# A max-pool-and-subtract stream with eight-row tiles in three slots instead of six-row tiles in four

## The chip, the cores and the metric

The kernel runs on one core of a Trainium2 chip. The metric is the device time of that core in microseconds; the profile's span, from the first to the last recorded instruction, is some 2 us shorter than the run it was taken in (624.8 us against 626.6 us). Lower is better.

The parts of the core that matter here: VectorE (DVE) does all arithmetic; SyncE (SP) issues the loads and ScalarE (ACT) the stores, each on a queue of its own; sixteen DMA engines, shared by both queues, move the data; TensorE (PE) only passes on a semaphore.

## What is computed

An array of 8 x 64 images of 256 x 256 float32 numbers. Each image is cut into windows of 8 x 8, the maximum of each window is taken, and every element has the maximum of its window subtracted:

```python
def reference(x):
    B, C, H, W = x.shape          # 8, 64, 256, 256
    pH, pW = 8, 8
    oH, oW = H // pH, W // pW
    x_r = x.reshape(B, C, oH, pH, oW, pW)
    pooled = x_r.max(axis=(3, 5))
    upsampled = np.repeat(np.repeat(pooled, pH, axis=2), pW, axis=3)
    return (x - upsampled).astype(np.float32)
```

134.22 MB come in and as much goes out.

## The kernel before

A "row" in this kernel is a strip of eight image lines, 2048 numbers or 8 KB, which holds 32 whole windows and is contiguous in memory. There are 16,384 of them, 128 for each of the 128 partitions. They are worked in tiles: a first tile of four rows per partition, 20 tiles of six, and a last tile of four. A tile of six rows takes for each partition one contiguous run of 48 KB, so one descriptor of the transfer moves 48 KB. The first tile comes in two loads and leaves in two stores, the last one leaves in three.

```python
ROW = 2048
HEAD, HEAD_OUT = [3, 1], [2, 2]
SIZE, TILES = 6, 20
TAIL = [2, 1, 1]
SLOTS = 4
...
    sizes = [sum(HEAD)] + [SIZE] * TILES + [sum(TAIL)]
    last = len(sizes) - 1
    ring = data.tile([P, SLOTS * SIZE * ROW], F32, name="ring")
    tops = data.tile([P, SLOTS * SIZE * oW], F32, name="tops")
```

`ring` is a ring of slots in SBUF, 24 rows or 192 KB per partition. Tile i lies in slot (i - 1) % SLOTS. The subtraction is done in place: a tile is loaded into its slot, changed there, and stored from there, so a slot is taken from the start of a load to the end of the store.

The load queue. A load into a slot that was used before waits until the stores of the tile that lay there have landed (L113 of the profile is the issue of a load):

```python
        for i in range(len(sizes)):
            slot = slot_of(i)
            if landed[slot]:
                nc.sync.wait_ge(stored[slot], 16 * landed[slot])
            for k, (lo, R) in enumerate(cuts(HEAD if i == 0 else [sizes[i]])):
                part = slice(lo * ROW, (lo + R) * ROW)
                nc.sync.dma_start(out=sbuf(i, lo, R), in_=dram(x_rows, i)[:, part]).then_inc(
                    first[k] if i == 0 else loaded[slot], 16
                )
            landed[slot] += len(HEAD_OUT) if i == 0 else 1
```

TensorE turns "this tile has landed" into one step of a single semaphore, `filled`, which the loop on VectorE can wait for with a constant:

```python
        for i in range(1, last):
            turn = (i - 1) // SLOTS + 1
            nc.tensor.wait_ge(loaded[slot_of(i)], 16 * turn).then_inc(filled, 1)
```

The store queue waits for VectorE's `ready` and issues the store (L130):

```python
        for i in range(len(sizes)):
            for lo, R in cuts(HEAD_OUT if i == 0 else TAIL if i == last else [SIZE]):
                part = slice(lo * ROW, (lo + R) * ROW)
                done += 1
                nc.scalar.wait_ge(ready, done)
                nc.scalar.dma_start(out=dram(out_rows, i)[:, part], in_=sbuf(i, lo, R)).then_inc(
                    stored[slot_of(i)] if i + SLOTS <= last else final, 16
                )
```

VectorE: for each tile one reduction over all its windows (L81) and one subtraction per row (L96); the tile counts as ready after the last subtraction. `take` (L75) waits for a semaphore and counts it down.

```python
        nc.vector.tensor_reduce(out=..., in_=..., axis=mybir.AxisListType.XY, op=mybir.AluOpType.max,
        ).then_inc(reduced if nth is None else pooled, 1)
        ...
        for r in range(R):
            sub = nc.vector.tensor_tensor(
                out=wins[:, r],
                in0=wins[:, r],
                in1=maxs[:, r].unsqueeze(1).unsqueeze(3).to_broadcast([P, pH, oW, pW]),
                op=mybir.AluOpType.subtract,
            )
        sub.then_inc(ready, 1)
...
        with nc.vector.Fori(0, TILES) as i:
            slot = i % SLOTS
            take(filled, 1)
            pool_and_subtract(
                ring[:, bass.ds(slot * (SIZE * ROW), SIZE * ROW)],
                tops[:, bass.ds(slot * (SIZE * oW), SIZE * oW)],
                SIZE,
            )
```

Of the kernel before, what the change touches and what calls it, by code (L numbers as in the profile page):

```python
# [1 line left out]

# [4 lines left out]

F32 = mybir.dt.float32
ROW = 2048


HEAD, HEAD_OUT = [3, 1], [2, 2]
SIZE, TILES = 6, 20
TAIL = [2, 1, 1]
SLOTS = 4


@with_exitstack
def kernel(
    ctx: ExitStack,  # L20
    tc: tile.TileContext,
    x: bass.AP,
    out: bass.AP,
):
    nc = tc.nc
    P = nc.NUM_PARTITIONS
    B, C, H, W = x.shape
    pH = pW = 8
    oW = W // pW

    x_rows = x.rearrange("b c (oh ph) w -> (b c oh) (ph w)", ph=pH)
    out_rows = out.rearrange("b c (oh ph) w -> (b c oh) (ph w)", ph=pH)
    sizes = [sum(HEAD)] + [SIZE] * TILES + [sum(TAIL)]
    assert sum(sizes) * P == x_rows.shape[0] and max(sizes) == SIZE
    starts = [P * sum(sizes[:i]) for i in range(len(sizes))]
    last = len(sizes) - 1

    data = ctx.enter_context(tc.tile_pool(name="data", bufs=1))
    ring = data.tile([P, SLOTS * SIZE * ROW], F32, name="ring")
    tops = data.tile([P, SLOTS * SIZE * oW], F32, name="tops")  # L40
    first = [tc.alloc_semaphore(f"first{i}") for i in range(len(HEAD))]
    loaded = [tc.alloc_semaphore(f"loaded{i}") for i in range(SLOTS)]
    stored = [tc.alloc_semaphore(f"stored{i}") for i in range(SLOTS)]
    final = tc.alloc_semaphore("final")
    filled = tc.alloc_semaphore("filled")
    reduced = tc.alloc_semaphore("reduced")
    pooled = tc.alloc_semaphore("pooled")
    ready = tc.alloc_semaphore("ready")

    def slot_of(i):  # L50

        return (i - 1) % SLOTS

    def dram(rows, i):

        n = sizes[i]
        return rows[starts[i] : starts[i] + P * n].rearrange("(p r) d -> p (r d)", r=n)

    def sbuf(i, lo, R):
        at = (slot_of(i) * SIZE + lo) * ROW  # L60
        return ring[:, at : at + R * ROW]

    def top(i, lo, R):
        at = (slot_of(i) * SIZE + lo) * oW
        return tops[:, at : at + R * oW]

    def cuts(parts):
        lo = 0
        for R in parts:
            yield lo, R  # L70
            lo += R

    def take(sem, n):

        nc.vector.wait_ge(sem, n).then_inc(sem, -n)  # L75

    def pool_and_subtract(part, top, R, nth=None):

        wins = part.rearrange("p (r ph ow pw) -> p r ph ow pw", r=R, ph=pH, ow=oW)
        maxs = top.rearrange("p (r ow) -> p r ow", r=R)  # L80
        nc.vector.tensor_reduce(  # L81
            out=maxs if R > 1 else maxs[:, 0],
            in_=(
                wins.rearrange("p r ph ow pw -> p r ow ph pw")
                if R > 1
                else wins[:, 0].rearrange("p ph ow pw -> p ow ph pw")
            ),
            axis=mybir.AxisListType.XY,
            op=mybir.AluOpType.max,
        ).then_inc(reduced if nth is None else pooled, 1)  # L90
        if nth is None:
            take(reduced, 1)
        else:
            nc.vector.wait_ge(pooled, nth)
# [9 lines that stand above are left out]
    with tc.tile_critical(sync_engine=nc.gpsimd.engine, no_gpsimd_drain=True):  # L104

        landed = [0] * SLOTS
# [17 lines that stand above are left out]
        done = n_final = 0  # L124
# [8 lines that stand above are left out]
                n_final += i + SLOTS > last  # L133
        nc.scalar.wait_ge(final, 16 * n_final)


        for k, (lo, R) in enumerate(cuts(HEAD_OUT)):
            nc.vector.wait_ge(first[[a + n >= lo + R for a, n in cuts(HEAD)].index(True)], 16)
            pool_and_subtract(sbuf(0, lo, R), top(0, lo, R), R, k + 1)
# [8 lines that stand above are left out]
        nc.vector.wait_ge(loaded[slot_of(last)], 16 * ((last - 1) // SLOTS + 1))  # L148
        for k, (lo, R) in enumerate(cuts(TAIL)):
            pool_and_subtract(sbuf(last, lo, R), top(last, lo, R), R, len(HEAD_OUT) + k + 1)  # L150


# [1 line left out]
_INS = ['x']  # L154
_OUTS = [((8, 64, 256, 256), 'float32')]


# [23 lines left out]
```

## Time and profile before

| | |
|---|---|
| time, median of 3 runs | 627.52 us (627.07 to 628.71) |
| span of the profiled run | 624.8 us |
| moved, in and out | 268.44 MB, mean 430 GB/s |
| VectorE busy | 560.2 us, of which reductions 276.8 and subtractions 284.1 |
| one reduction of six rows | 12.95 us |
| one subtraction of a row | 2.287 us |
| a load of six rows per partition, issue to landing (median) | 37.9 us |
| a store of six rows per partition, issue to landing (median) | 51.0 us |

The page gives busy time by engine, then forty equal slices of the span: a digit is the busy share of a slice in tenths, and for DMA it is the mean share of the core's sixteen engines; GB/s is what they moved. Lists of waits name the waiting engine and line, what ended the wait, and then the total in us, how often, and the longest. In a table by stretches each row has the stretch, its length, busy time of VectorE and of GpSimd with instruction counts, the granted clock, the DMA share and GB/s. The timeline has start, length, engine, line and operation, and in brackets the idle time before.

### The profile page before, as it was taken

How to read it: one execution, taken by the hardware profiler on the slowest of the kernel's cores; microseconds unless marked ns; L12 is line 12 of the kernel's file. 1: busy time of each engine (PE TensorE's matmuls, PEld its weight loads, DVE VectorE, ACT ScalarE, POOL GpSimd, SP SyncE). 2: the span in 40 equal slices, each digit the busy share in tenths (PEclk: the TensorE clock that was granted, in tenths of full speed). 3: DMA queues.
4: the chain of work that ended last, by engine and by line, in shares of the span. 5: the costliest groups of instructions: out<-in, count | busy, mean ns of one | idle time of the engine just before them, and what ended most of it. 6: DMA issues, size and time to landing. Idle time of an engine off the chain costs nothing. (4 is left out here: it accounts for less than half of the span.)

```text
span 624.8 us, 519 instructions
## 1 busy us (share of the span) xinstructions
DVE 560.2 (90%) x153; POOL 0.2 (0%) x4
## 2 busy tenths in 40 slices
DVE  3899999999999898989898989889898989898991
POOL 0000000000000000000000000000000000000000
DMA  9999999999999999999999999999999999999998
GB/s 369 415 447 413 453 403 453 450 406 453 428 428 450 406 453 441 415 453 419 437 450 406 453 431 425 453 403 453 444 412 453 425 431 447 409 453 432 441 422 350
DMA packets 6913, 268.44 MB, mean 430 GB/s; under 512 B 769, under 2 KB 769, under 8 KB 769
## 3 DMA queue, kind: packets, MB, share of 16 engines
q1 hardware_dynamic: 3312, 134.22, 49.9%
q10 hardware_dynamic: 3600, 134.22, 49.7%
q14 instruction: 1, 0.00, 0.0%
HBM read 134.22 MB, written 134.22 MB: 430 GB/s over the span
## 5 line engine op out<-in xcount | busy, mean ns | idle before, releaser
L81 DVE TENSOR_REDUCE tops<-ring (+2 forms) x25 | 276.8, 11074 | 47.4 <-DVEq L75 36.7
L96 DVE TENSOR_TENSOR ring<-ring,tops (+1 forms) x128 | 284.1, 2287 | 3.3 <-DVEq L75 3.1
L165 POOL MEMSET const-bfloat16-1.0<- 128x1 bf16 x1 | 0.1, 102 | 0.0
L165 POOL MEMSET const-uint8-127<- 128x1 uint8 x1 | 0.1, 102 | 0.0
L165 POOL MEMSET const-float32-0.0<- 128x1 f32 x1 | 0.1, 99 | 0.2 <-issue 0.2
L165 POOL MEMSET const-float32-1.0<- 128x1 f32 x1 | 0.1, 99 | 0.0
## 6 DMA issues: line engine op xcount, KB each, us to landing
ring<-in_x_dram SPq DMA_DIRECT2D x20, 6144.0 KB, 37.9
out_dram<-ring ACTq DMA_DIRECT2D x20, 6144.0 KB, 51.0
out_dram<-ring ACTq DMA_DIRECT2D x3, 2048.0 KB, 24.8
ring<-in_x_dram SPq DMA_DIRECT2D x1, 4096.0 KB, 33.4
ring<-in_x_dram SPq DMA_DIRECT2D x1, 3072.0 KB, 9.8
out_dram<-ring ACTq DMA_DIRECT2D x2, 1024.0 KB, 13.8
ring<-in_x_dram SPq DMA_DIRECT2D x1, 1024.0 KB, 11.9
```

Source lines behind the costliest of these rows:

```text
L81: nc.vector.tensor_reduce(out=maxs if R > 1 else maxs[:, 0], in_=(wins.rearrange("p r ph ow pw -> p r ow ph pw") if R > 1 else wins[:, 0]. ...
L96: sub = nc.vector.tensor_tensor(out=wins[:, r], in0=wins[:, r], in1=maxs[:, r].unsqueeze(1).unsqueeze(3).to_broadcast([P, pH, oW, pW]), op ...
L165: nc = _bacc.Bacc("TRN2", target_bir_lowering=False, num_devices=1)
```

## The change

The tiles between the first and the last have eight rows in place of six, so that each partition's part of one is 64 KB, and there are 15 of them in place of 20. To fit the same 24 rows of SBUF, there are three slots in place of four. The first tile's four rows come in two loads of two rows, in place of three and one. The purpose is to have fewer transfers and larger descriptors, 64 KB in place of 48. Nothing else in the text of the kernel changes; the waits follow from the constants: a load of tile i now waits for the store of tile i - 3.

```diff
-HEAD, HEAD_OUT = [3, 1], [2, 2]
-SIZE, TILES = 6, 20
+HEAD, HEAD_OUT = [2, 2], [2, 2]
+SIZE, TILES = 8, 15
 TAIL = [2, 1, 1]
-SLOTS = 4
+SLOTS = 3
```

## The prediction

> **What bounds the kernel now.** I read the page first (busy shares, slices, queues), then the time by stretches, then the wait lists of VectorE and of the load queue, and last the timeline of both ends. The page alone names two candidates:
>
> ```profile
> span 624.8 us, 519 instructions
> DVE 560.2 (90%) x153; POOL 0.2 (0%) x4
> ...
> DMA  9999999999999999999999999999999999999998
> GB/s 369 415 447 413 453 403 453 450 406 453 428 428 450 406 453 441 415 453 419 437 450 406 453 431 425 453 403 453 444 412 453 425 431 447 409 453 432 441 422 350
> ...
> q1 hardware_dynamic: 3312, 134.22, 49.9%
> q10 hardware_dynamic: 3600, 134.22, 49.7%
> ```
>
> VectorE is busy for 90% of the span, but the sixteen DMA engines are busy for all of it: loads (q1) and stores (q10) share them half and half, 99.6% together. The stretches say the same without the two ends:
>
> ```profile
> 0.00:30.00 30.00, 17.74 (x6) 0.20 (x4) 1.00 0.95 387
> 30.00:600.00 570.00, 531.62 (x143) 0.00 (x0) 1.00 1.00 434
> 600.00:624.80 24.80, 10.83 (x5) 0.00 (x0) 1.00 0.91 391
> ```
>
> The last two columns are the DMA share and GB/s. For 570 us the share is 1.00 at 434 GB/s. All 268.44 MB at that rate take 618.5 us, so of the 624.8 only about 6 us are not transfer at the full rate. The packet records of the trace begin at 1.9 and end at 623.2 with no hole. Who waits for whom:
>
> ```profile
> DVE tops L81 <- DVEq L75: 36.7, 15, 2.7
> DVE tops L81 <- DMA ring<-in_x_dram: 10.7, 1, 10.7
> ...
> SPq L113 <- DMA out_dram<-ring: 547.7, 18, 60.6
> ```
>
> VectorE's wait at L75 is its wait for a load, up to 2.7 us on 15 tiles: it keeps up and waits for data. The load queue waits for stores (L113, `stored`). And yet DMA never idles, since issued stores stand in line: from issue to landing a 6 MB store takes 51.0 us and a load 37.9, where one alone would take 14.5 (6.29 MB at 434). That line is the reserve of four slots. The chain of waits shows 5% only, all VectorE at the end; it does not see transfers, so it is no help here.
>
> **What the Trainium skill says.** "DMA: Bandwidth & Descriptors", section "Where 436 GB/s comes from", gives a ceiling of 435.2 GB/s for the sixteen engines; the 434 above agrees, so there is nothing left in the middle for larger descriptors to win. The same page, "Queues, rings and completion order", says each engine takes turns between the queues that have work; the trace agrees: with both queues full, a 48 KB load descriptor (1.815 us) and a store descriptor alternate, and each transfer takes about twice its time alone. Its section "Anatomy of one DMA" says that a wait for a semaphore is made by the issuing sequencer, not by the DMA engine; so a load whose slot is not free is not in any queue, and an engine can go dry. No wait of that kind ends in an idle DMA in the trace before.
>
> **The change part by part.** *Descriptors.* The packet records have 8 KB in 0.309 us and 48 KB in 1.815 us: 36.8 ps a byte and 8 ns fixed. 2,560 descriptors of 48 KB in each direction become 1,920 of 64 KB, on each engine 320 become 240; 80 x 8 ns = 0.6 us gained.
>
> *VectorE's work* is the same: 128 subtractions at 2.287 us and the same rows reduced. From one reduce to the next of a six-row tile it is 26.32 us (30.75 to 57.07 in the timeline), so eight rows take 35.0. A tile's two transfers take 8 x 2 x 2.416 = 38.7 us (a row of all partitions is 1.0486 MB, 2.416 us at 434 GB/s), so VectorE at 35.0 stays below the DMA. The order of instructions shows no other change than shapes, counts and two more subtractions in the loop's body.
>
> *Slots.* SBUF holds the same 24 rows. In the loop of one slot stand load, VectorE, store and three latencies. I take from the trace: last load packet to reduce 2 us (0.85 from the last engine, plus that the engines end up to 2.2 us apart), last subtraction to first store packet 2 us (1.0 idle, 3.6 under load), last store packet to first packet of the load that waits for it 2.5 us (0.36 to the semaphore, 1.0 to the first packet, and half of the 2.4 us between engines). With full queues the round is 37 + 2 + 35 + 2 + 37 + 2.5 = 115.5 us against 3 x 38.7 = 116. Four slots of six: 27 + 2 + 26.3 + 2 + 27 + 2.5 = 87 against 4 x 29.0 = 116. A reserve of 29 us becomes one of nothing. Holes appear where neither a load nor a store is ready, so I schedule by hand, both queues sharing evenly when both have work:
>
> Start: two rows land at 6.7, VectorE works 7.6 to 25.4 on tile 0. The first eight-row tile lands at 40.6 (sixteen row transfers, 38.7, after 1.9), and VectorE starts on it at 42.6 (before: 30.75). From there VectorE runs tiles 1 to 5 back to back, ending at 77.6, 112.6, 147.6, 182.6, 217.6. Loads 2 and 3 end at 79.3; store 1 runs alone from 79.6 to 98.9, then load 4 may start, at 101.4: hole of 2.5. Load 4 is alone until store 2 at 114.6; store 2 ends 140.0, load 5 at 142.5: hole 2.5. Store 3 ends 181.2, load 6 at 183.7: hole 2.5. Store 4 ends 222.4 with store 5 in line: no hole. Start together, with 0.3 before store 1: 7.8.
>
> Middle: from here stores and loads end within 2 us of each other, and one of them nearly always bridges the other's gap; going on in the same way to tile 14, I find holes of 1.0, 0.9, 0.3 and 0.8: 3.0.
>
> End: load 15 lands at 572.7, VectorE works on it until 609.7. All that DMA has meanwhile is store 14 (19.3) and the four-row load 16 (9.7), done by 602.5. Store 15 begins at 610.7: hole of 8.2. Before, loads end near 588 and two full stores stand in line behind, so no hole.
>
> Sum: 7.8 + 3.0 + 8.2 = 19.0, less 0.6 for descriptors, 18.4 on the span. The time before, 627.5, becomes 645.9, slower by 2.9%.
>
> **The rivals.** *The transfers hide it all:* VectorE still has 3.7 us a tile to spare and some transfer is nearly always open; then only the descriptors count: 627. For it speaks the 99.6%, against it the reserve worked out above and the end, where one tile of VectorE's work is longer than what is left to move. *Every tile has a hole:* loads and stores fall into step, both end together, and each of twelve steady tiles idles for the 2.5 us from store to load: 30 us in place of 3, about 672. For it: both rounds, 115.5 and 116, are equal within my error. Against it: VectorE's spare time lets the next store be in line already. *Large descriptors run faster:* the 36.8 ps a byte at 8 KB and at 48 KB alike speak against more than 1 us, 626.
>
> **Range and chances.** The end's hole is the surest part (it rests on 35.0 us of VectorE against 29.0 of transfers plus latencies), say 5 to 11 us; the start's 4 to 10; the middle 0 to 15. Holes can also be partly bridged where the sixteen engines end at different times, so there is more room below. Low: 636; high: 654. The 2% line is at 640.1, 5.8 below my number, so slower by over 2% gets 0.76, within 2% 0.23, faster 0.01.
>
> **What would show it.** Right: VectorE's first eight-row reduce near 42 us; slices with a DMA digit of 8 or less or GB/s near 380 in the first third and one clear dip near 605 us; DMA share of the two queues together about 97%; VectorE busy again 560 us; shorter times from issue to landing, stores most. Steady stretches at 430 GB/s or more say that the middle costs nothing. Wrong: a span near 625 with all nines (the reserve was not needed), GB/s below 420 in every slice of the middle (holes at each tile), or full DMA digits at lower GB/s, which would mean that 64 KB descriptors themselves are slower, which nothing here foretells.

## The result and the profile after

The changed kernel takes 651.70 us (median) against 627.75 us before: ratio 1.0379, 95% interval 1.0361 to 1.0396. It is slower by 3.8%; predicted was 645.9 us, 2.9%. Times here are medians of all executions; the ratios leave out slow ones, of which there was one in four for this kernel (679.78 us), for six rows in three slots (666.93 us) and for "the end alone" (658.67 us).

The same lines of the page, now of the changed kernel: span, VectorE, DMA by slices, the two queues, then from its last part the eight-row transfers with the median time from issue to landing.

```profile
span 649.8 us, 469 instructions
DVE 559.2 (86%) x148; POOL 0.2 (0%) x4
...
DMA  9999998999999999999999999999899999999697
GB/s 387 452 403 371 387 452 323 452 391 448 452 432 407 436 387 440 420 432 444 424 424 391 391 452 452 436 403 448 335 452 440 424 428 440 452 365 413 266 444 331
...
q1 hardware_dynamic: 2592, 134.22, 49.6%
q10 hardware_dynamic: 2880, 134.22, 47.8%
...
ring<-in_x_dram SPq DMA_DIRECT2D x15, 41.2
out_dram<-ring ACTq DMA_DIRECT2D x15, 41.6
```

VectorE does the same work (559.2 us). The bytes are the same, the span is 25.0 us longer. The digits hardly tell: 9 nearly everywhere, since a transfer that is open but slow counts as busy. GB/s tells: dips to 323, 335 and 266. An eight-row store lands 41.6 us after its issue; a six-row one took 51.0. The line of issued stores is gone: 41.6 us is 2.2 times the 19.3 us that one such store takes alone, where 51.0 was 3.5 times 14.5.

The wait lists, VectorE's and the load queue's, in the same columns as before:

```profile
DVE tops L81 <- DVEq L75: 65.8, 13, 10.9
...
SPq L113 <- DMA out_dram<-ring: 572.8, 14, 59.8
```

VectorE waits for loads for 65.8 us in place of 36.7, up to 10.9 at a time.

Stretches of the changed kernel, cut where GB/s drops. Columns: stretch, length, VectorE and GpSimd busy, clock, DMA share, GB/s.

```profile
60.00:80.00 20.00, 20.00 (x7) 0.00 (x0) 1.00 0.94 365
...
104.00:112.00 8.00, 8.00 (x3) 0.00 (x0) 1.00 0.81 262
112.00:220.00 108.00, 95.87 (x26) 0.00 (x0) 1.00 1.01 437
220.00:231.00 11.00, 9.87 (x3) 0.00 (x0) 1.00 0.97 340
231.00:340.00 109.00, 95.00 (x26) 0.00 (x0) 1.00 1.00 433
340.00:351.00 11.00, 9.99 (x3) 0.00 (x0) 1.00 0.89 316
351.00:458.00 107.00, 93.05 (x25) 0.00 (x0) 1.00 1.00 431
458.00:469.00 11.00, 10.15 (x4) 0.00 (x0) 1.00 0.86 304
469.00:580.00 111.00, 98.52 (x27) 0.00 (x0) 1.00 1.00 434
580.00:589.00 9.00, 7.73 (x2) 0.00 (x0) 1.00 0.97 342
...
610.00:620.00 10.00, 10.00 (x5) 0.00 (x0) 1.00 0.26 111
```

Between the dips the rate is that of before, 431 to 437 GB/s. So 64 KB descriptors are not slow; the loss lies in the dips. I count a dip as lost transfer: its length times (1 - GB/s / 434), from the packet records with each packet's bytes spread over its duration. (The table's GB/s puts bytes a little differently at the edges of a stretch.) Start, to 113 us: 2.5 + 1.2 + 3.6 = 7.3 us. Middle, around 227, 346, 423, 465 and 584: 2.5 + 2.8 + 0.4 + 2.8 + 2.4 = 10.9. End, around 615: 7.0. The sum is 25.2 us; the spans differ by 25.0. What is left in either kernel, at the first and last bytes above all, is alike: 4.7 us in the changed one, 4.9 in all in the kernel before. So the dips are the whole difference.

The timeline of the changed kernel, of which I show only reductions (start, length, engine, line, operation, idle time before):

```profile
37.04 17.22 DVE L81 TENSOR_REDUCE tops<-ring  x1 [10.86 <-DVEq L75]
...
188.83 17.22 DVE L81 TENSOR_REDUCE tops<-ring  x1 [8.52 <-DVEq L75]
...
308.73 17.22 DVE L81 TENSOR_REDUCE tops<-ring  x1 [8.53 <-DVEq L75]
...
428.46 17.22 DVE L81 TENSOR_REDUCE tops<-ring  x1 [8.64 <-DVEq L75]
...
546.56 17.22 DVE L81 TENSOR_REDUCE tops<-ring  x1 [8.60 <-DVEq L75]
...
582.91 17.22 DVE L81 TENSOR_REDUCE tops<-ring  x1 [1.27 <-DVEq L75]
...
617.91 4.41 DVE L81 TENSOR_REDUCE tops<-ring 128x64 f32<-128x4096 f32 x1
```

The pattern repeats after three tiles, one turn of the three slots: 188.83 to 308.73 is 119.9 us, to 428.46 another 119.7, to 546.56 another 118.1. Three tiles' transfers take 116.0 at 434 GB/s. And the last eight-row tile holds VectorE from 582.91 to 617.9; the transfers open at 582.91 were done by 612.5, so DMA stood nearly empty until its store could begin.

### The profile page after: what moved, and what is told of

It reads as the page before. It is cut to its first block, busy times and chain, and to the rows that moved or that the text cites. A ratio compares the mean times of both kernels' runs of the same rounds, so it can differ in the third digit from the quotient of the medians.

```text
span 649.8 us, 469 instructions
## 1 busy us (share of the span) xinstructions
DVE 559.2 (86%) x148; POOL 0.2 (0%) x4
## 5 line engine op out<-in xcount | busy, mean ns | idle before, releaser
L81 DVE TENSOR_REDUCE tops<-ring (+2 forms) x20 | 276.1, 13804 | 74.2 <-DVEq L75 65.8
## 6 DMA issues: line engine op xcount, KB each, us to landing
ring<-in_x_dram SPq DMA_DIRECT2D x15, 41.2
out_dram<-ring ACTq DMA_DIRECT2D x15, 41.6
```

The lines of the kernel that those rows point to most:

```text
L81: nc.vector.tensor_reduce(out=maxs if R > 1 else maxs[:, 0], in_=(wins.rearrange("p r ph ow pw -> p r ow ph pw") if R > 1 else wins[:, 0]. ...
```

## The experiments

The theory, "slots": with three slots, the round of one slot (load, VectorE, store, latencies) is as long as the transfers of three tiles, so that a queue runs dry now and then. The rivals: the descriptors' size; the bytes held in SBUF; transfers that are simply slower. All edits are to the changed kernel. A ratio is to the kernel before, measured beside it, with its 95% interval.

**Slots without the size.**

```diff
-SIZE, TILES = 8, 15
+SIZE, TILES = 6, 20
 SLOTS = 3
```

> Slots alone: six-row tiles (48 KB descriptors, as before) in three slots. Theory 'slots' (the round of a slot, load + VectorE + store + latencies, no longer fits with room to spare): 27 + 2 + 26.3 + 2 + 27 + 2.5 = 87 us against 3 x 29 = 87, so about as slow as the change, 641 to 652 us. Rival 'descriptors' (64 KB descriptors are what costs): 626 to 630 us.

Measured: 655.12 us, ratio 1.0408 (1.0350 to 1.0466), a little slower than expected. From 60 to 600 us:

```profile
60.00:600.00 540.00, 470.12 (x127) 0.00 (x0) 1.00 1.00 417
```

The descriptors of before, with three slots, have the whole loss, here in more and smaller dips (in the packet records none in the middle costs over 1.9 us, the end 4.6). So 64 KB descriptors are not needed for it. This kernel also holds fewer rows, 18; the next run takes that up.

**Four slots with less memory.**

```diff
-SIZE, TILES = 8, 15
+SIZE, TILES = 5, 24
-SLOTS = 3
+SLOTS = 4
```

> Five-row tiles in four slots, 20 rows of SBUF, less than the 24 of both kernels. Theory 'slots': four slots leave some 20 us of reserve, so 625 to 631 us. Rival 'buffered bytes' (only the rows held in SBUF count): slower than before, 640 us or more.

Measured: 626.70 us, ratio 0.9995 (0.9988 to 1.0002). In its page's slices the DMA digits are all nines again up to the last slice:

```profile
DMA  9999999999999999999999999999999999999998
GB/s 384 389 448 449 419 419 461 419 419 461 419 419 461 419 419 461 419 419 461 419 422 459 419 422 459 419 425 456 419 430 451 419 433 448 419 435 429 450 422 352
```

20 rows in four slots do what 24 rows in three cannot. It is not the bytes held. GB/s in slices still varies between 419 and 461 with no loss, as in the kernel before: a slice alone proves no dip.

**The size without the slots.** Each load and store of an eight-row tile goes out as two transfers of four rows (32 KB descriptors), under the same waits:

```diff
-cuts(HEAD if i == 0 else [sizes[i]])
+cuts(HEAD if i == 0 else [sizes[i] // 2] * 2)
...
+                for at, n in [(lo, R // 2), (lo + R // 2, R // 2)] if R == SIZE else [(lo, R)]:
```

> The changed kernel with each load and store of eight rows issued as two transfers of four rows under the same waits, so that descriptors are 32 KB. Theory 'slots': nothing of the round changes, 647 to 653 us; the stretch of slow transfer where the store queue starts anew may shrink a little if it goes with the size of a descriptor. Rival 'descriptors': back to 626 to 632 us.

Measured: 653.48 us, ratio 1.0403 (1.0375 to 1.0430). Halving the descriptors gives nothing back.

**VectorE's part of the round.** Four, two or one of the eight subtractions of each loop tile are left out; those rows are stored unchanged. Loads, stores and waits remain.

```diff
-        for r in range(R):
+        for r in range(R if nth else R // 2):     # or R - 2, or R - 1
```

> The changed kernel with four of the eight subtractions of each loop tile left out (the other four rows are stored unchanged): VectorE's part of the round falls from 35.0 to 26.2 us, transfers and waits stay. Theory 'slots': the round gets 9 us of reserve, holes in the middle and at the end go, 627 to 634 us. Rivals 'descriptors' and 'DMA is the only limit, and slower': 648 to 653 us.

Measured: 635.07 us, ratio 1.0124 (1.0087 to 1.0160). Stretches of that run:

```profile
60.00:80.00 20.00, 20.00 (x3) 0.00 (x0) 1.00 1.00 396
...
112.00:590.00 478.00, 318.83 (x61) 0.00 (x0) 1.00 1.00 433
590.00:605.00 15.00, 14.77 (x6) 0.00 (x0) 1.00 0.77 330
```

The middle has no loss left (433 GB/s over 478 us; the changed kernel has 424 over 112 to 589). The start keeps 3.4 us of loss and, against the expectation, the end 5.0 of its 7.0; so the time is 1 us above the stated range. So 16.6 of the 24 us come back when VectorE's part shrinks, with every byte and wait in place; a slower DMA by itself is ruled out.

> The same with two of the eight subtractions left out, VectorE's part 30.6 us. Theory: round 114.6, so no hole in the middle; start (6 us) and end (5 us) stay: 636 to 641 us. Rival: 646 to 652 us.

Measured with two left out: 640.20 us, ratio 1.0216 (1.0198 to 1.0234), as expected for the time. The middle has nearly no loss left:

```profile
80.00:590.00 510.00, 398.46 (x92) 0.00 (x0) 1.00 1.00 431
```

The loss is 3.7 us at the start and, more than the 5 expected, 7.4 at the end.

> The changed kernel with one of the eight subtractions of each loop tile left out (that row is stored unchanged): VectorE's part of the round 32.8 us. Theory 'slow start of a store' (a store that meets a running load takes 5.5 us to its first packet, where 2 was predicted, so the round of the changed kernel is 119 us and not 115.5): the round becomes 116.8 against 116, so most of the 11 us lost in the middle go, 639 to 645 us. Rival 'the round fits anyway, the middle is lost for another reason': only the end gains up to 2 us, 649 to 652 us.

Measured with one left out: 650.47 us, ratio 1.0345 (1.0285 to 1.0406), its runs scattered from 645.5 to 654.5. That missed the theory's range and lies in the rival's, but for another reason than the rival's: the losses of its profiled run (the slowest, 654.5 us) lie in the middle, up to 6 us in one place around 330 us, so the middle did not stay as it was. Its semaphore counts show one thing that changed: from the first to the last of the sixteen engines of one transfer up to 13.4 us pass. In the kernel before that is 2.5 at most, in the changed one 5.7. A load waits for all sixteen counts of the store before it, so for the slowest engine. That this makes the round longer near the limit, and different from run to run, is my reading; no run isolates it. This run decides nothing between theory and rival; the one with two left out met the theory's range and not the rival's.

**Fewer slots still.**

```diff
-SLOTS = 3
+SLOTS = 2
```

> Eight-row tiles in two slots. Theory 'slots': while VectorE has one slot (35 us) the other must store and load (19.3 + 2.5 + 19.3 + 2 = 43 us), so about 43 to 45 us a tile in place of 39.9, 690 to 725 us. Rival 'descriptors': little above 652 us.

Measured: 694.29 us in a single run beside 626.95, at the low end. With two slots each queue starts from empty at every tile, which shows the cost of such a start by itself. The timeline of this run around two starts:

```profile
515.21 42.77 SPq L113 DMA_DIRECT2D ring<-in_x_dram  x2
530.80 45.88 ACTq L130 DMA_DIRECT2D out_dram<-ring  x2
541.23 17.22 DVE L81 TENSOR_REDUCE tops<-ring  x1 [10.46 <-DVEq L75]
```

The load is issued at 515.21 when the store before has landed; the next store at 530.80, while the load is running alone. In the packet records that store's first packet is at 537.2, 6.4 us after its issue, and from 534 to 537 the load falls to some 305 GB/s: 1.1 us lost. Where a store is issued and nothing else runs (618.0 in the changed kernel), 0.84 us pass. A load that is issued with everything empty starts after 0.95 us, but with the landing and a slow first descriptor (3.0 to 3.2 us in place of 2.4) costs 2.3 to 2.7 us of transfer in this run.

**The end alone.** The last eight-row tile is reduced, subtracted and stored in four pieces of two rows.

```diff
+LATE = [2, 2, 2, 2]
-        with nc.vector.Fori(0, TILES) as i:
+        with nc.vector.Fori(0, TILES - 1) as i:
+        for i, parts in ((last - 1, LATE), (last, TAIL)):   # each part: reduce, subtract, ready
```

> The changed kernel, but the last eight-row tile is reduced, subtracted and stored in four pieces of two rows. Theory: the hole before the last big store (7.0 us of lost transfer in the changed kernel) goes, since the first piece is ready after 9 us and not after 35: 643 to 646.5 us. If that hole was only moved to another place: 650 to 652 us.

Measured: 644.73 us, ratio 1.0272 (1.0252 to 1.0293). The stretch that had 111 GB/s in the changed kernel now reads

```profile
610.00:620.00 10.00, 9.96 (x4) 0.00 (x0) 1.00 0.99 424
```

The hole at the end was 7.0 us, and 7.0 us came back in the medians. The profiled spans differ by 6.1 only (649.8 and 643.7), since this run lost 0.6 us more in its middle.

**The head alone.**

```diff
-HEAD, HEAD_OUT = [2, 2], [2, 2]
+HEAD, HEAD_OUT = [3, 1], [2, 2]
```

> The changed kernel with the first tile loaded in three rows and one, as before the change. Theory: this part of the change does nothing that lasts: 650 to 654 us. Rival: the even head is part of the loss, 645 us or less.

Measured: 649.98 us, ratio 1.0379 (1.0343 to 1.0415), the changed kernel's ratio. This part of the change does nothing that shows.

**The other direction.**

```diff
-SIZE, TILES = 8, 15
+SIZE, TILES = 4, 30
-SLOTS = 3
+SLOTS = 6
```

> Other direction: four-row tiles in six slots, the same 24 rows, 32 KB descriptors. Theory 'slots': round 19 + 2 + 17.5 + 2 + 19 + 2.5 = 62 us against 6 x 19.3 = 116, so no holes: 624 to 629 us. Rival 'larger transfers are better': slower than before.

Measured: 627.90 us, ratio 1.0010 (1.0002 to 1.0017). No dips. With 32, 40 or 48 KB to a descriptor and four slots or more the time is the same within 0.2%; none of these beats the kernel before by more than 0.1%.

**A repair with three slots.** The loads keep 64 KB; a tile is stored in pieces as its rows get ready, first four of two rows, then two of four.

```diff
-        sub.then_inc(ready, 1)
+            if nth is None and r % 2 or r == R - 1:      # two pieces: r % 4 == 3
+                sub.then_inc(ready, 1)
-cuts(... else [SIZE])
+cuts(... else [2] * (SIZE // 2))                         # two pieces: [4] * (SIZE // 4)
```

> Repair that keeps three slots and 64 KB loads: each eight-row tile is stored in four transfers of two rows, each issued as soon as its two rows are subtracted (16 KB descriptors). Theory 'slots': the first piece can go after 17.2 + 4.4 = 21.6 us in place of 35, and most of the tile is already out when VectorE is done, so the slot is held for about 92 us against 116 and the store queue never stands empty; the end's hole goes too: 626 to 632 us. Rival: smaller store descriptors and four times as many stores cost what is won, 640 us or more.

Measured: 642.93 us, ratio 1.0232 (1.0194 to 1.0270): a miss. The dips of the middle are gone, but the end of the run reads

```profile
600.00:610.00 10.00, 10.00 (x5) 0.00 (x0) 1.00 1.00 428
...
630.00:645.30 15.30, 0.00 (x0) 0.00 (x0) 1.00 0.15 61
```

At 61 GB/s for the last 15 us, after VectorE has finished: in the packet records what moves from 632 to 644 us is 27 GB/s, a sixteenth of 434: a single engine works off its share of the last stores. First and last engine of one store lie up to 30 us apart.

> The changed kernel with each eight-row tile stored in two transfers of four rows, each issued when its four rows are subtracted: the first after 17.2 + 8.8 = 26 us in place of 35, the end's hole (7.0 us) largely gone. The run with four pieces lost 14 us at its end on DMA engines that had fallen behind the others. Theory 'many transfers pull the engines apart': with half as many the engines stay closer, 630 to 638 us. Rival 'tight slots alone pull them apart': 639 to 647 us, as with four pieces.

Measured: 631.33 us, ratio 1.0055 (1.0039 to 1.0070).

```profile
80.00:590.00 510.00, 470.61 (x122) 0.00 (x0) 1.00 1.00 433
```

The engines stay within 3.5 us of each other, the only losses over 1 us are 2.8 for the first bytes (as before) and 3.2 at the start of the eight-row stores. 20 of the 24 us come back with 64 KB loads and three slots. It is not the smaller stores: in "the size without the slots" the same two stores of four rows, issued together after the last subtraction, gave nothing. It was the time that a slot is held.

## Why the prediction was right or wrong

*What bounds the kernel, and that the descriptors matter little.* Right. The rate between dips is unchanged, and the runs with halved and with smaller descriptors show no effect of size. The 0.6 us to be won is below what can be seen. The section of the Trainium skill that the prediction cites for 435.2 GB/s ("DMA: Bandwidth & Descriptors", "Where 436 GB/s comes from") also says that HBM holds transfers between HBM and SBUF to about 358; the 434 measured here, with one core at work, is above that, and the measurement decides.

*A reserve of 29 us becomes nothing.* Right as a mechanism: slots alone make the loss, four slots of fewer rows undo it, and a shorter stay of VectorE's work or an earlier store undoes most of it.

*Start: 7.8 us.* Measured 7.3, in part by luck: three holes of 2.5 were predicted, and 2.5, 1.2 and 3.6 came. The times were off too: the first eight-row reduction began at 37.04 and not near 42. I let both queues share evenly; the first tile's stores have 16 KB descriptors beside loads of 64, and in the packet records from 22 to 62 us 192 of the loads' descriptors began and 256 of the stores', so that the loads moved three quarters of the bytes.

*Middle: 3.0 us.* Wrong in size; it measured 10.9. These 7.9 us, less 0.5 and 1.2 at the two ends, are the miss of the whole (5.8 us in the median, 6.6 in the profiled span). The step that failed is the round of a slot, 115.5 us. In the packet records of the changed kernel the rounds of tiles 4 to 12 are 119.1 us in the mean:

| part of the round | predicted | measured (mean) |
|---|---|---|
| load, first packet to last landing | 37 | 37.5 |
| landing to reduce | 2 | 0.9 |
| VectorE | 35 | 35.1 |
| last subtraction to first store packet | 2 | 4.1 |
| store, first packet to last landing | 37 | 37.8 |
| landed store to first packet of the next load | 2.5 | 3.7 |

The most mis-sized term is "last subtraction to first store packet 2 us (1.0 idle, 3.6 under load)": the figure lies between the two, though running loads are the usual case here. In the changed kernel a store that starts from an empty queue beside running loads took 4.2 to 6.3 us. In the middle that is one tile in three (tiles 5, 8, 11 and 14, each at one of the large dips); the other stores were issued while the one before was still open. The start of the load after a store comes next. No run changes these latencies by themselves; that the round is what counts is shown by the runs above, its parts by the trace alone.

The second half of the error is "one of them nearly always bridges the other's gap": it does, but at 304 to 342 GB/s, not at 434. So the middle loses little in holes where nothing is ready; it loses most in stretches of 8 to 10 us in which a load runs nearly alone, and slowly, while the store queue starts. The spread among the engines, which I put at 2.4 us, reached 5.7; it is part of the two transfers in the table. The run with one subtraction less shows that a sum of such terms is no sharp limit.

*End: 8.2 us.* Measured 7.0, and taken out by itself it gave 6 to 7 us back.

*The rivals.* The transfers did not hide it all. A hole at every tile did not come, it is one in three; the reason given against it, VectorE's spare time, held for two tiles of three.

*Signs in the profile.* The two queues' shares, 97.4%, and VectorE's 559 us came as said, the dip at the end too (266 GB/s). Digits of 8 or less were a poor sign: only four of the forty slices have one, the lowest two (6 and 7) at the end. The time from issue to landing became shorter for stores (51.0 to 41.6 us) but not for loads (37.9 to 41.2); only against the time of one alone, 14.5 and 19.3 us, did it fall for both.

What stays open: why a load running alone slows down while a store is starting, and what pulls the sixteen engines apart. Both are seen here, neither is explained. That two pieces stay together and four do not fits the number of transfers as a cause, or their smaller descriptors (16 KB against 32), but it is two runs and not a proof.

## What to carry to other kernels

Before making tiles larger at the cost of slots, add up how long one slot is held (load, work, store, each transfer at the shared rate, and the latencies under load) and set it against slots times the time per tile; keep a spare of more than the latencies, since near equality the time gets longer and scatters (645.5 to 654.5 us in the run with one subtraction left out). If the slots cannot be had, store a tile in two parts as it gets ready; here that came to within 0.6% of the kernel before. Look at GB/s over stretches and at the line of issued transfers (time from issue to landing against the time of one alone): the busy digits of DMA stay at nine through most of such a loss.

## What the runs showed of the hardware that was not expected

A queue that starts from empty is quick on idle engines (0.84 to 1.0 us from issue to first packet) and slow beside the other queue: in the runs with 48 and 64 KB descriptors 3.6 to 6.6 us for a store beside loads and 3.4 to 4.8 us for a load beside stores; with 32 KB descriptors in three slots 3.5 to 4.5 us for a store and 3.6 to 3.8 for a load. The store beside a load that runs alone costs transfer too, about 1.1 us each time in the run with two slots; a load that joins stores shows no dip of its own in the changed kernel. And the sixteen engines are not in step: 0.9 us at most from first to last with five rows in four slots, 2.5 in the kernel before, 13 and 30 us in two of the runs with three slots. A spread alone costs nothing where there is time to spare: with four subtractions left out it is up to 6.8 us, and the middle runs at 433 GB/s.
